# MLP handover, last attention units, and the layer-1 attention loop with its projection in single matmuls and its last fold in halves

## The chip, the cores and the metric

The kernel runs on one core of a Trainium2 chip. The metric is the device time of one execution in microseconds (us). PE is the matmul engine, DVE (VectorE), ACT (ScalarE) and POOL (GpSimd) are the elementwise engines, and SP is the queue from which all DMAs are issued. Each engine runs its own instructions in a fixed order and waits on semaphores.

## The reference, cut to what matters

Two layers of a diffusion transformer over 1024 latent tokens and 256 context tokens, width 1024, in float32:

```
for layer in range(2):
    h_l, h_c = modulate(x, norm1), modulate(ctx, norm1)
    layer 0: y_c, y_l = ab_mixer(h_c, h_l)        # mLSTM + windowed attention
    layer 1: y_l = c_mixer(h_c, h_l)              # full attention, 8 heads, 2 kv heads
    x = x + mod_l[2] * y_l
    x = x + mod_l[5] * (relu(modulate(x, norm2) @ w1) ** 2 @ w2)
    layer 0 only: the same two steps for ctx
return x

c_mixer:  q, k = rms_norm(q), rms_norm(k); rope for the latent ones
          k_all = [k_ctx, k_lat]; v_all = [v_ctx, v_lat]          # 1280 keys
          o = softmax(q k_all^T / sqrt(128)) v_all; y_l = o @ w_out
```

## The kernel before, in words

**High and low parts.** Every float32 operand of PE is kept as a rounded high part and the rest, its low part. `split` makes them: ACT copies the high part (L397), then DVE or POOL subtracts it from the source (L398). A product is three matmuls: high x high, high x low, low x high. A weight tile lands in a raw buffer by DMA and is then split into one of the buffers `W0_105`, `W1_106`, `W2_4594` to `W5_4597`.

**The MLP.** Both matrix products use a seven-product scheme on 2 x 2 blocks of operands. In the first one, `pair` computes two 128-wide hidden blocks from seven products (11, S1, 12, S2, 22, S3, S4). DVE combines the products out of PSUM (L643, "evacuations"), ACT applies the squared relu (`finish`, L600 and L601), and the results and sums of them go to DRAM (`hd`): `column_sums` and `row_sums` add blocks on DVE (L618) and store them (L619). `direct` (two matmul groups and a finish) does the context tokens of layer 0. Pairs 14 and 15 are in an order written out by hand. In the last pair the generator `ahead` is stepped once per `step()`: it loads and splits the operands of the first three steps of the second product, on POOL. This is the handover. `pending["row"]` holds the row sums of a pair; they run in the next pair, and their stores must land before their buffers are used again by that pair.

**The second product**, `mlp_out`, walks the hidden blocks in four stages ("14", "56", "27", "3"). A step is 24 matmuls (L1046) on operands that `mlp_feed` loads ahead (L924), adds (L969) and splits on DVE. The scheduler orders this part by its own model of time. The residual `x` is loaded from `xs` two tiles per step (L1119) and results are added to it on DVE (L1051).

**Layer 1's attention.** A unit is one head h and one tile t of 256 query tokens; 32 units run in an order written out by hand, and each iteration k works on three units: scores and maxima of k, values of k-1, division of k-2. Scores of the 1280 keys fill five PSUM banks of 512 columns (two chunks of 256 keys each, L423 to L425 through `mm3`). DVE folds them into a running maximum u.m, 512 wide (L1965), and at last merges its two halves (L1968). Two PE transposes (L1992), a reduction (L1994), two more transposes (L1998) and an ACT copy (L2002) bring the negative maximum to the layout of the scores; `shift` adds it (L2008). `weigh` takes the exponential on ACT (L2027 high part, L2028 in full) and the low part on POOL (L2029). `values` multiplies by V (L2017) into a bank that the chain of transposes uses too, so it waits for L2002. The sum of the exponentials is collected in ACC (`total1` copies on ACT, L1976; `total2` and `total3` add on DVE), `total4` sums it over partitions on PE (L2020), `divide1` takes its reciprocal by Ln and Exp on ACT (L2033, L2034), and `divide2` multiplies (L2038). Between these PE runs the query projection of unit k+2 as filler: `project` is a generator of 24 matmuls (L1924), and `run(fill, n)` takes n steps of it. The order on PE around it is

```
on(fold, k, 4, NB); fill = project(k + 2); run(fill, 5)
on(maxima1, k); run(fill, 2)
on(maxima2, k); on(total2, k - 1); run(fill, 2)
on(shift, k); on(values, k - 1, 0)
```

**The end of attention.** In the last six units `early` starts the output projection: it loads output weights (`load_wo`) and finished heads (`load_first`, from DRAM), splits them (`split_wo` on POOL, `split_first` on DVE or POOL) and runs their products as filler (`out`, L2079). Its table is keyed by unit (counted from the end) and place in the unit: -6 is k = 26, -1 is k = 31, and 0 and 1 are the two iterations after it.

## Time and profile before

| | us |
|---|---|
| three runs | 2779.29, 2780.57, 2788.60 |
| median | 2780.57 |
| the profiled execution | 2788.63 |
| its span, first to last instruction | 2786.8 |
| PE busy | 2695.9 (97%) |
| DVE, ACT, POOL busy | 1885.0, 1476.7, 1095.2 |
| mean granted PE clock | 0.992 |

Rows of a timeline have the start, the duration, engine, line, operation, names and shapes, a count, and in brackets the idle time ahead of it and what ended it. Layer 0's handover lies near 1200 to 1222 us, layer 1's attention loop between 1690 and 2068, layer 1's handover near 2472.

### The profile page before, as it was taken

The numbers are of one execution on the slowest core, as the hardware profiler recorded it, in microseconds if no ns is written. First come the engines' busy times: TensorE is split into PE (matmuls) and PEld (weight loads), VectorE is DVE, ScalarE is ACT, GpSimd is POOL, SyncE is SP. The second block draws the span as 40 slices with busy tenths as digits, with TensorE's granted clock in tenths as the row PEclk, the third lists the DMA queues.
The fourth block names the chain that finished last, engine by engine and source line by source line (L and its number), as shares of the span: only waits on it lengthen the run. The fifth ranks groups of instructions, "written<-read, shape, count | busy, mean of one in ns | idle before, by whom it ended". The sixth has DMA issues, their size and how long they took to land.

```text
span 2786.8 us, 40782 instructions
## 1 busy us (share of the span) xinstructions
PE 2695.9 (97%) x14683; PEld 2284.5 (82%) x14683; DVE 1885.0 (68%) x3268; ACT 1476.7 (53%) x2611; POOL 1095.2 (39%) x744
## 2 busy tenths in 40 slices
PE   6899999999999999999999999999999999999999
PEld 3688788878788888878878889999988888888877
DVE  4645655677876766557678757888874677666676
ACT  4654554445564444344436557888865554444432
POOL 3430220000237576530001346787865499740000
PEclk9999999999999999999999999999999999999999
DMA  7122233363335667488756710000045155577664
GB/s 241 56 84 100 79 104 112 108 210 99 110 108 174 209 220 237 157 307 286 246 166 218 243 61 26 24 28 20 26 150 195 65 174 192 175 284 263 215 223 154
DMA packets 194659, 428.33 MB, mean 154 GB/s; under 512 B 21128, under 2 KB 47336, under 8 KB 194456
## 3 DMA queue, kind: packets, MB, share of 16 engines
q1 hardware_dynamic: 194456, 425.73, 45.6%
q8 instruction: 115, 1.88, 0.3%
q14 instruction: 88, 0.72, 0.1%
HBM read 322.90 MB, written 102.74 MB: 153 GB/s over the span
## 4 chain that ended last, share of the span: by engine, by line
PE 73%; DVE 6%; DMA 4%; issue 3%; ACT 2%; POOL 1%; DVEq 0%; SPq 0%; POOLq 0%; ACTq 0%
PE psum L588 21%; PE psum L1046 17%; PE psum L423 4%; PE psum L2017 4%; PE psum L424 4%; PE psum L425 4%; PE psum L2203 3%; PE psum L1142 3%; PE psum L1924 3%; DMA hhiraw<-in_w 2%; DVE W L398 2%; POOL W L398 1%; PE psum L1500 1%; PE psum L2079 1%; PE psum L1506 1%
## 5 line engine op out<-in xcount | busy, mean ns | idle before, releaser
L398 POOL TENSOR_TENSOR W<-F,W 128x512 fp32r<-128x512 f32 (+2 forms) x319 | 489.1, 1547 | 519.4 <-ACT W L397 438.8
L1046 PE MATMUL psum<-W,W 128*128 128x512 f32 x2688 | 617.8, 391 | 10.9 <-DVE W L398 4.7
L1046 PEld LDWEIGHTS psum<-W,W 128*128 128x128 f32 x2688 | 504.6, 188 | 123.6 <-DVE W L398 10.9
L588 PE MATMUL psum<-hhi,W 128*128 128x512 f32 (+1 forms) x1600 | 442.2, 356 | 2.3 <-DVE x L1774 0.9
L397 ACT ACTIVATE W<-F 128x512 fp32r<-128x512 f32 (+2 forms) x380 | 275.1, 739 | 292.6 <-POOL F L561 99.4
L588 PEld LDWEIGHTS psum<-hhi,W 128*128 128x128 f32 x1600 | 285.1, 189 | 46.3 <-issue 2.5
L588 PE MATMUL psum<-hlo,W 128*128 128x512 f32 (+1 forms) x800 | 284.3, 355 | 0.0
L397 ACT ACTIVATE W<-hhiraw 128x1024 fp32r<-128x1024 f32 x98 | 104.0, 1061 | 316.2 <-PE psum L1046 235.4
L423 PE MATMUL psum<-hhi,W 128*128 128x512 f32 (+1 forms) x624 | 232.8, 373 | 0.9 <-ACT F L1432 0.9
L424 PE MATMUL psum<-hlo,W 128*128 128x512 f32 (+1 forms) x624 | 227.3, 364 | 0.0
L425 PE MATMUL psum<-hhi,W 128*128 128x512 f32 (+1 forms) x624 | 227.1, 364 | 0.0
L969 DVE TENSOR_TENSOR hhiraw<-hhiraw 128x512 f32<-128x512 f32 x154 | 108.3, 712 | 108.4 <-DMA hhiraw<-in_w 107.6
L561 POOL TENSOR_TENSOR F<-F 128x512 f32<-128x512 f32 x112 | 164.8, 1471 | 13.5 <-DMA F<-in_w 4.5
L588 PEld LDWEIGHTS psum<-hlo,W 128*128 128x128 f32 x800 | 151.2, 189 | 21.4 <-issue 0.2
L390 POOL TENSOR_TENSOR hlo<-F,hhi 128x512 fp32r<-128x512 f32 (+1 forms) x24 | 27.4, 1144 | 347.6 <-ACT F L381 347.6
L398 DVE TENSOR_TENSOR W<-hhiraw,W 128x1024 fp32r<-128x1024 f32 x98 | 119.6, 1221 | 60.7 <-ACT W L397 58.2
L423 PEld LDWEIGHTS psum<-hhi,W 128*128 128x128 f32 x624 | 118.4, 190 | 21.3 <-ACT x L397 2.5
L424 PEld LDWEIGHTS psum<-hlo,W 128*128 128x128 f32 x624 | 118.5, 190 | 17.3 <-issue 2.2
L425 PEld LDWEIGHTS psum<-hhi,W 128*128 128x128 f32 x624 | 118.3, 190 | 17.3 <-issue 0.5
L588 PE MATMUL psum<-x,W 128*128 128x512 f32 x504 | 123.5, 389 | 0.0
L398 DVE TENSOR_TENSOR W<-hloraw,W 128x1024 fp32r<-128x1024 f32 x98 | 119.4, 1218 | 0.7 <-ACT W L397 0.7
L2203 PE MATMUL psum<-W,W 128*128 128x512 f32 (+1 forms) x408 | 109.5, 372 | 2.4 <-POOL W L398 1.5
(450 smaller groups left out, 6231.2 us busy)
## 6 DMA issues: line engine op xcount, KB each, us to landing
F<-in_w SPq DMA_DIRECT2D x104, 512.0 KB
hloraw<-hd SPq DMA_DIRECT2D x90, 512.0 KB
hhiraw<-in_w SPq DMA_DIRECT2D x72, 512.0 KB
hd<-F SPq DMA_DIRECT2D x142, 256.0 KB
hhiraw<-in_w SPq DMA_DIRECT2D x116, 256.0 KB
F<-in_ada_w SPq DMA_DIRECT2D x96, 256.0 KB
hd<-x SPq DMA_DIRECT2D x90, 256.0 KB
F<-in_win SPq DMA_DIRECT2D x33, 512.0 KB
```

What stands on the lines that cost most here:

```text
L397: nc.scalar.activation(hi, src, AF.Copy)
L398: eng.tensor_tensor(lo, src, hi.bitcast(F32), op=ALU.subtract)
L423: nc.tensor.matmul(ps, sh, mh, start=i == 0, stop=False)
L424: nc.tensor.matmul(ps, sh, ml, start=False, stop=False)
L425: nc.tensor.matmul(ps, sl, mh, start=False, stop=i == n - 1)
L561: add = lambda o, p, q, how: nc.gpsimd.tensor_tensor(o, p, q, op=how)
L588: nc.tensor.matmul(ps, w[i][:, p], B[j][k], start=first and j == 0 and m == 0, stop=last and j == 3 and m == 2)
L969: tt = lambda o, p, q, how: eng.tensor_tensor(o, p, q, op=how)
L1046: nc.tensor.matmul(bank(base + i), A[u][:, p], B[v], start=first and m == 0, stop=last and m == 2)
L1142: nc.tensor.matmul(bank(k), B[u][:, i * P : i * P + P], A[v][:, half], start=f == 0 and m == 0, stop=f == NFF - 1 and m == 2,)
L2017: nc.tensor.matmul(u.o[:, :QT], v[x], p[y], start=c == 0 and m == 0, stop=c == 2 * NB - 1 and m == 2)
L2203: self.nc.tensor.matmul(ps, x[:, c], y, start=first and m == 0, stop=last and m == 2)
```

## The change

It has five parts. (1) In pair 15 the row sums of pair 14 run before product S1 instead of after it. (2) In `ahead` the low parts of the first step's hidden operand and the whole split of the second step's weights go from POOL to DVE. (3) The loads of x keep their program order in SP's queue, and the loads of kind "3" are issued behind the last of them in layer 0. (4) In the attention loop the projection yields after each matmul, and the fills between fold, first transposes, second transposes and values are 11, 5 and 8 matmuls instead of 15, 6 and 3 (the ninth step of the last fill takes the square of the finished projection). The fold's last block is taken in two 256-wide halves before the merge, and `divide1` stands before `total1`. (5) In the last units `split_wo(0)` moves from the start of unit 27 to behind its shift; heads 5 and 6 are staged in a free part of F and loaded in unit 30, and head 5 is split there on POOL instead of on DVE in unit 31.

```diff
@@ pair
             step()
+            if b == NFF // 2 - 1:
+                pending.pop("row")()
             ps = bank()
             prod(ps, A["S1"], T1)
@@ ahead
-            feed.split_b(0, eng)
+            feed.split_b(0, nc.vector)
             feed.load_a(2)
             yield
             feed.load_b(1)
-            feed.split_a(1, eng)
+            feed.split_a(1, nc.vector)
@@ mlp_feed
-        def load(t, src):
-            nc.sync.dma_start(t if len(src.shape) == 2 else t.rearrange("p (k n) -> p k n", k=src.shape[1]), src)
+        def load(t, src, behind=False):
+            t = t if len(src.shape) == 2 else t.rearrange("p (k n) -> p k n", k=src.shape[1])
+            with self.tc.issue_after(fd.mark.ins) if behind and hc else nullcontext():
+                nc.sync.dma_start(t, src)
...
@@ mlp_out
-                        nc.sync.dma_start(self.x[j][:, t0 : t0 + n], save[:, j, t0 : t0 + n])
+                        feed.mark = self.tc.keep_in_program_order(
+                            nc.sync.dma_start(self.x[j][:, t0 : t0 + n], save[:, j, t0 : t0 + n])
+                        )
@@ project
-                yield
+                    yield
@@ fold
-            for b in range(b0, b1):
+            for b in range(b0, min(b1, NB - 1)):
                 nc.vector.tensor_tensor(u.m, u.S[:, b * 512 : b * 512 + 512], u.m, op=ALU.max)
             if b1 < NB:
                 return
+            for i in range(2):
+                m, c = u.m[:, i * QT : i * QT + QT], 2 * NB - 2 + i
+                nc.vector.tensor_tensor(m, u.S[:, c * QT : c * QT + QT], m, op=ALU.max)
             nc.vector.tensor_tensor(u.m[:, :QT], u.m[:, :QT], u.m[:, QT:], op=ALU.max)
@@ load_first
-                stage[j] = aw.tile([P, H], F32, tag="mix", bufs=2)
+                if j in (5, 6):
+                    stage[j] = self.F[:, 2 * PG + (j - 5) * H : 2 * PG + (j - 4) * H]
+                else:
+                    stage[j] = aw.tile([P, H], F32, tag="mix", bufs=2)
@@ early
-                (-5, 0): ((split_wo, 0), (load_first, 0, 1)),
+                (-5, 0): ((load_first, 0, 1),),
+                (-5, 2): ((split_wo, 0),),
...
-                (-2, 0): ((load_wo, 2),),
+                (-2, 0): ((load_wo, 2), (load_first, 5, 6)),
...
-                (-2, 2): ((split_first, 3, V), (split_first, 4, G), (load_first, 5, 6)),
+                (-2, 2): ((split_first, 3, V), (split_first, 4, G), (split_first, 5, G)),
...
-                (-1, 3): ((split_first, 5, V), (out, 0, (5,))),
+                (-1, 3): ((out, 0, (5,)),),
@@ the loop
+                on(divide1, k - 2)
                 on(total1, k - 1)
-                on(divide1, k - 2)
...
-                run(fill, 5)
+                run(fill, 11)
...
-                run(fill, 2)
+                run(fill, 5)
                 on(maxima2, k)
                 on(total2, k - 1)
-                run(fill, 2)
+                run(fill, 9)
```

Three places in the order of instructions. First PE in an attention unit, from the last of the projection's matmuls ahead of the first transposes to the values. Before:

```order
6836 L1924 MATMUL psum<-hhi,W_4597 128x256
6837 L1992 MATMUL psum<-ident,F 128x128 x2
6838 L1924 MATMUL psum<-hhi,W_4597 128x256
6839 L1924 MATMUL psum<-hlo,W_4597 128x256
6840 L1924 MATMUL psum<-hhi,W_4597 128x256 x2
6841 L1924 MATMUL psum<-hlo,W_4597 128x256
6842 L1924 MATMUL psum<-hhi,W_4597 128x256
6843 L1998 MATMUL psum<-ident,F 128x128 x2
6844 L1924 MATMUL psum<-hhi,W_4597 128x256
6845 L1924 MATMUL psum<-hlo,W_4597 128x256
6846 L1924 MATMUL psum<-hhi,W_4597 128x256
6847 L2017 MATMUL psum<-x_13158,x_12916 128x256
```

In the changed kernel, whose line numbers are a few higher:

```order
6792 L2001 MATMUL psum<-ident,F 128x128 x2
6793 L1930 MATMUL psum<-hhi,W_4597 128x256 x2
6794 L1930 MATMUL psum<-hlo,W_4597 128x256
6795 L1930 MATMUL psum<-hhi,W_4597 128x256 x2
6796 L2007 MATMUL psum<-ident,F 128x128 x2
6797 L1930 MATMUL psum<-hlo,W_4597 128x256
6798 L1930 MATMUL psum<-hhi,W_4597 128x256 x2
6799 L1930 MATMUL psum<-hlo,W_4597 128x256
6800 L1930 MATMUL psum<-hhi,W_4597 128x256 x2
6801 L1930 MATMUL psum<-hlo,W_4597 128x256
6802 L1930 MATMUL psum<-hhi,W_4597 128x256
6803 L2026 MATMUL psum<-x_13158,x_12916 128x256
```

Five matmuls of the projection moved from ahead of the second transposes to behind them; four of them from ahead of the first.

Second DVE at layer 0's handover, from the evacuation of h11 of pair 15 (`x_7127` and `x_7126` are its temporaries, `W_105` and `W_106` operands of the second product). Before:

```order
1608 L643 TENSOR_TENSOR x_7127<-psum,x_7126 128x512
1609 L643 TENSOR_TENSOR x_7126<-psum,x_7126 128x512 x2
1610 L643 TENSOR_TENSOR x_7126<-x_7126,psum 128x512
1611 L643 TENSOR_TENSOR x_7126<-psum,x_7126 128x512
1612 L643 TENSOR_TENSOR F<-psum,x_7126 128x512
1613 L643 TENSOR_TENSOR x_7126<-psum,x_7126 128x512
1614 L618 TENSOR_TENSOR F<-x_7126,x_7127 128x512
```

In the changed kernel:

```order
1608 L643 TENSOR_TENSOR x_7127<-psum,x_7126 128x512
1609 L398 TENSOR_TENSOR W_105<-F,W_105 128x1024
1610 L643 TENSOR_TENSOR x_7127<-psum,x_7127 128x512
1611 L643 TENSOR_TENSOR x_7126<-psum,x_7126 128x512
1612 L973 TENSOR_TENSOR F<-F 128x512
1613 L398 TENSOR_TENSOR W_106<-F,W_106 128x1024
1614 L643 TENSOR_TENSOR x_7126<-x_7126,psum 128x512
1615 L643 TENSOR_TENSOR x_7126<-psum,x_7126 128x512
1616 L643 TENSOR_TENSOR F<-psum,x_7127 128x512
1617 L643 TENSOR_TENSOR x_7127<-psum,x_7127 128x512
```

Two low parts and an add came from POOL and stand between the evacuations of S2 (rows 1610 and 1611) and that of product 22 (row 1614).

Third POOL in units 29 to 31 (`hlo` is the low part of a finished head, `W_4597` an output weight). Before:

```order
468 L398 TENSOR_TENSOR hlo<-F,hhi 128x512
469 L2029 TENSOR_TENSOR x_13160<-x_13163,x_13158 128x1280
470 L1941 TENSOR_TENSOR F<-F 128x256
471 L1942 TENSOR_TENSOR F<-F 128x256
472 L2029 TENSOR_TENSOR x_13161<-F,x_13159 128x1280
473 L398 TENSOR_TENSOR W_106<-F,W_105 128x256
474 L398 TENSOR_TENSOR hlo<-F,hhi 128x512
475 L2029 TENSOR_TENSOR W_106<-x_13162,W_105 128x1280
476 L398 TENSOR_TENSOR W_4597<-F,W_4597 128x1024
```

In the changed kernel:

```order
465 L398 TENSOR_TENSOR hlo<-F,hhi 128x512
466 L2038 TENSOR_TENSOR x_13160<-x_13163,x_13158 128x1280
467 L1947 TENSOR_TENSOR F<-F 128x256
468 L1948 TENSOR_TENSOR F<-F 128x256
469 L2038 TENSOR_TENSOR x_13161<-F,x_13159 128x1280
470 L398 TENSOR_TENSOR W_106<-F,W_105 128x256
471 L398 TENSOR_TENSOR hlo<-F,hhi 128x512 x2
472 L2038 TENSOR_TENSOR W_106<-x_13162,W_105 128x1280
```

POOL splits a second finished head (x2) ahead of the low part of a unit's weights.

8 lines of the change are left out of this document (4 added, 4 removed).

## The prediction

> **What bounds the kernel now.** First the busy rows, then windows by stage, then PE's waits.
>
> ```profile
> PE 2695.9 (97%) x14683; PEld 2284.5 (82%) x14683; DVE 1885.0 (68%) x3268; ACT 1476.7 (53%) x2611; POOL 1095.2 (39%) x744
> ...
> 1200.00:1222.00 22.00, 16.55 (x72) 12.88 (x71) 11.62 (x13) 11.05 (x17) 13.11 (x7) 0.84 0.73 248
> 1222.00:1244.00 22.00, 22.00 (x99) 18.22 (x98) 15.32 (x16) 9.18 (x10) 1.67 (x1) 1.00 1.03 388
> 1712.00:2000.00 288.00, 284.46 (x2244) 275.41 (x2243) 249.66 (x391) 235.05 (x373) 226.98 (x152) 1.00 0.08 25
> ...
> PE psum L1046 <- DVE W L398: 4.7, 8, 0.9
> PE psum L1046 <- POOL W L398: 1.1, 1, 1.1
> ```
>
> PE bounds it: the change removes no matmul, so only PE's pauses can move. Columns of the windows: length, then busy time of PE, PEld, DVE, ACT, POOL, the granted clock. Layer 0's handover (1200 to 1222) lacks 5.5 us of PE and runs at clock 0.84; the 22 us behind it lack none (99 matmuls, 0.222 us each). The attention loop lacks 3.5 us in 288 (24 units of some 12 us); what its last units lack stands with term 2. The two wait rows are layer 1's output stage (4.7 us) and its handover (1.1).
>
> **Term 1, the attention loop.** One ordinary unit (last score matmul at S = 1947.27), then a unit near the end with no projection, whose chain nothing covers:
>
> ```profile
> 1947.27 0.28 PE L425 MATMUL psum<-W,hb 128*128 128x256 f32 x1
> 1947.47 0.41 DVE L2038 TENSOR_TENSOR F<-psum,F 128x256 f32<-128x256 f32 x1
> 1947.81 0.68 DVE L1965 TENSOR_TENSOR F<-psum,F 128x512 f32<-128x512 f32 x1
> 1948.52 0.43 DVE L1968 TENSOR_TENSOR F<-F 128x256 f32<-128x256 f32 x1
> 1949.19 0.39 PE L1992 MATMUL psum<-ident,F 128*128 128x128 f32 x2
> 1949.58 2.95 POOL L2029 TENSOR_TENSOR x<-x,x 128x1280 fp32r<-128x1280 f32 x1 [1.67 <-ACT x L2028]
> 1950.12 0.40 PE L1998 MATMUL psum<-ident,F 128*128 128x128 f32 x2
> 1950.56 0.38 ACT L2002 ACTIVATE F<-psum 128x256 f32<-128x256 f32 x1 [0.75 <-PE psum L1998]
> 1950.99 0.98 PE L2017 MATMUL psum<-W,x 128*128 128x256 f32 x6
> ...
> 2044.31 0.42 DVE L1968 TENSOR_TENSOR F<-F 128x256 f32<-128x256 f32 x1
> 2044.88 0.41 PE L1992 MATMUL psum<-ident,F 128*128 128x128 f32 x2 [0.16 <-DVE F L1968]
> 2045.82 0.41 PE L1998 MATMUL psum<-ident,F 128*128 128x128 f32 x2
> 2046.71 0.74 PE L2017 MATMUL psum<-x,x 128*128 128x256 f32 x4 [0.47 <-ACT F L2002]
> ...
> 1908.36 0.42 DVE L1985 TENSOR_TENSOR F<-psum,F 128x256 f32<-128x256 f32 x1
> 1908.82 0.42 DVE L1986 TENSOR_TENSOR F<-psum,F 128x256 f32<-128x256 f32 x1
> ```
>
> Now PE fills exactly up to the transposes: 16 starts in 1.92 us (0.12 each) reach the first at S+1.92, six more and two transposes (0.93, so the pair costs 0.21) the second at S+2.85. Only before the values does it pause: three more would reach them at S+3.42, they start at S+3.72, and the second one 0.22 later instead of 0.12 (six last 0.98, the last of them 0.28), S+3.94. The bare chain: merge L1968 to transpose 0.57, to the second transpose 0.94, to the values 0.89.
>
> The halves begin where the fold did, S+0.54. A 256-wide operation lets an independent one start 0.34 later (L2038 to L1965) and a dependent one 0.46 later (L1985 to L1986). The merge starts at S+1.34 instead of 1.25: two starts cost 0.80 where one cost 0.71. The transpose can start at S+1.91; PE, now with 11 matmuls ahead of it, is there at S+1.44 and pauses 0.47. Behind it five matmuls and two transposes (0.81) don't cover the chain's 0.94: second transposes at S+2.85. Two transposes and eight matmuls then lead to S+4.02, past the chain (2.85 + 0.89 = 3.74), so the old pause is gone; the second value matmul starts at S+4.14. Against S+3.94 that is +0.20 a unit: one pause of 0.3 and its slow restart are exchanged for two of 0.47 and 0.13. I take this value because the rows behind it are of the same shape, engine and operands. Lower end: with the merge at S+1.14, 0.11 earlier than now, the second value matmul is at S+3.94 again, nothing lost. Upper end: the 0.10 of a slow restart after the new pause, +0.30.
>
> The Trainium skill (VectorE: DVE Perf Modes, The TRN2 errata) says that each instruction pays a fixed extra latency, a large tile once and small tiles each; its PSUM row, (120 + elements)/0.96 GHz, gives as an estimate 0.66 us for 512 and 0.39 for 256, +0.12 a unit against the +0.09 of the rows, which would add about 1 us to the loop's sum. The trace's 0.68 and 0.41 agree within 0.03.
>
> The swapped reciprocal: L2033 waits for the total's matmul, and L1976 filled that wait.
>
> ```profile
> 1945.53 0.59 PE L2020 MATMUL psum<-F,ones 128*128 128x256 f32 x2
> 1945.69 0.58 ACT L1976 ACTIVATE psum<-x 128x512 f32<-128x512 f32 x1
> 1946.22 0.36 ACT L2033 ACTIVATE F<-psum 128x256 f32<-128x256 f32 x1
> ...
> 1913.91 1.35 ACT L397 ACTIVATE W<-F 128x256 fp32r<-128x256 f32 x2
> 1915.16 0.36 ACT L2002 ACTIVATE F<-psum 128x256 f32<-128x256 f32 x1
> ```
>
> The total ends at 1946.12, so L2033 can't move up, and L1976 behind L2034 costs ACT its 0.53 less 0.05 of idle: 0.48. Queued behind it: both weigh exponentials, then POOL's L2029, then L2002. In ordinary units ACT idles 0.75 before L2002, which covers it; without that cover it would cost 0.48 there too. In the six units that split the next head's weights (t = 3, heads 0 to 5) L2002 follows L397 at once: +0.48 there. Loop: 22 x 0.20 + 6 x 0.48 = **+7.3**; ends 0 and, with 0.30, +9.5. Two units without projection only see the later merge, 2 x 0.09: **+0.2**.
>
> **Term 2, the last units.**
>
> ```profile
> 2006.89 2.40 POOL L398 TENSOR_TENSOR W<-F,W 128x1024 fp32r<-128x1024 f32 x1
> 2008.07 1.50 DVE L1968 TENSOR_TENSOR F<-F 128x256 f32<-128x256 f32 x1
> 2009.69 0.20 PEld L1992 LDWEIGHTS psum<-ident,F 128*128 128x128 f32 x2 [1.55 <-ACT F L2028]
> ...
> 2056.83 0.41 PE L1992 MATMUL psum<-ident,F 128*128 128x128 f32 x2 [0.16 <-DVE F L1968]
> 2057.74 2.96 DVE L398 TENSOR_TENSOR hlo<-F,hhi 128x512 fp32r<-128x512 f32 x1
> 2060.76 0.79 PE L2079 MATMUL psum<-hlo,W 128*128 128x512 f32 x1 [2.49 <-DVE hlo L398]
> 2062.87 1.01 PE L2017 MATMUL psum<-W,x 128*128 128x256 f32 x3 [0.47 <-ACT F L2002]
> ```
>
> In unit 27 the merge takes 1.50 instead of 0.43 beside POOL's weight split; PE waits 1.55. Moved behind the shift, that split (one ACT and one POOL instruction) mostly lies in POOL's idle time (1.67 us of it before one of a unit's two L2029 above), and its weights are needed only units later: **-1.5**. In unit 31 a split on DVE takes 2.96 beside POOL, and first transpose to values lasts 6.04 where unit 30 took 1.83: with chunk 5 split a unit earlier on POOL, PE finds it done: **-4.2**. What is late next is L2002, as in unit 30. If the cover is gone (POOL behind with its second split of that unit, or the staging in F holding up the output weight that used to be loaded there) half of the gain stays: ends -5.9 and -3. The two staging loads, moved up SP's queue, pass only mix and output-weight loads; I cost them at nothing, since the loop moves 25 GB/s.
>
> **Term 3, layer 0's handover.**
>
> ```profile
> 1201.13 1.89 DVE L643 TENSOR_TENSOR x<-psum,x 128x512 f32<-128x512 f32 x3 [6.71 <-DMA hd<-x]
> 1203.78 1.05 ACT L397 ACTIVATE W<-F 128x1024 fp32r<-128x1024 f32 x1
> 1207.66 3.11 PE L1046 MATMUL psum<-W,W 128*128 128x512 f32 x12
> 1212.62 1.04 ACT L397 ACTIVATE W<-F 128x1024 fp32r<-128x1024 f32 x1
> 1213.73 2.35 POOL L398 TENSOR_TENSOR W<-F,W 128x1024 fp32r<-128x1024 f32 x1 [1.66 <-ACT W L397]
> 1216.14 6.23 PE L1046 MATMUL psum<-W,W 128*128 128x512 f32 x16 [1.93 <-POOL W L398]
> L398 DVE TENSOR_TENSOR W<-hhiraw,W 128x1024 fp32r<-128x1024 f32 x98 | 119.6, 1221 | 60.7 <-ACT W L397 58.2
> ```
>
> Two of POOL's splits (2.35 us each) and an add go to DVE, where a split takes 1.22. But DVE's order now has them ahead of pair 15's evacuations, and each waits for ACT. The h11 evacuation at 1201.13 waited for the store of a row sum; the row sums come earlier now and no x loads stand behind them, so I move all that follows up by 0.6. ACT's high part of W_105 then ends at 1204.2, DVE's low part at 1205.5, the two evacuations queued behind it at 1206.7, the add at 1207.4, ACT's next high part at 1208.4, DVE's low part at 1209.7, and the evacuation of product 22 only at 1210.4. PE needs that one's bank after three matmuls: a pause of 2.6. Behind it come the evacuations of S3 and S4 (till 1212.3), and behind these ACT's finishes, W_4597's high part till 1215.4 and POOL's low part till 1217.8, which is later than the 1216.1 of now. By then 27 of the first 48 matmuls are done, where now 13 are. Now the other 35 end at 1216.1 + 35 x 0.222 + 2.4 (the slow clock: 16 recorded ones take 6.23) = 1226.3; then, 21 more end at 1217.8 + 4.7 = 1222.5, 3.8 earlier. But the pair after that needs two more low parts from POOL, ready at 1225.2, and PE waits 1.8 of the gain back: **-2.0**. Ends -8.9 (5.5 of idle, 2.4 of slow clock and 1 of slow restarts: no loss left) and +2 (the pauses add and the clock falls).
>
> The granted clock falls to 0.84 after pauses of 2.9 and 1.9 us. By the Trainium skill (TensorE: Matmul & The Clock Gate, Part 1: The HAM clock gate (the "warmup" mystery)) the clock halves after an idle window of about 3.4 us, so pauses of 2.6 and 1.5 with 4 us of work between would keep it full; if it fell anyway, 2.4 comes back and the term is +0.4.
>
> **Term 4, the rest.** Layer 1's handover loses its 1.1 to POOL but gets the same blocked evacuations: **-0.5**, ends -1.1 and +3. The x loads, two in each step of 24 matmuls (5.3 us), are all issued before the first stage ends; nothing. In the output stages DVE's 4.7 us may shift either way by 2.
>
> **Sum**: 7.3 + 0.2 - 1.5 - 4.2 - 2.0 - 0.5 = -0.7. Against the profiled execution (2788.6, of which the span is 2786.8) that is 2787.9; it lies 8.0 above the runs' median of 2780.6 and is as long as the longest of them. A difference carries over, so 2780.6 - 0.7, **2780**.
>
> **Rivals.** *Shorter chain*: the halves let the merge start early. At S+1.14 the loop costs nothing (2780 - 7.3 = 2772.7), at S+0.87 PE waits for no merge, the second value matmul is at S+3.67, and 28 x 0.27 comes off (2765). For: half the fold needs only the first score chunk. Against: DVE, not the scores, sets the start, S+0.54. *Free handover*: evacuations don't block, all 8.9 us come back: 2773. Against: DVE runs in order. *ACT late everywhere* (slower): the slip of 0.48 pushes L2029, ending at S+5.26, towards the second half of the values, which needs it at S+4.02 + 15 x 0.12 + 0.33 = S+6.15. It decides from a slip of 0.9; each 0.1 beyond costs 28 x 0.1, so 1.2 gives 2788. For: POOL is busy 227 of 288 us. Against: a slip of 0.48 leaves 0.41. *The moves earn nothing*: DVE waits for the store as before, and POOL or the staging is late in the last units; terms 2 and 3 are zero: 2780 + 7.7 = 2788. Against: both waits end on the instructions that are moved.
>
> **Numbers.** Forecast 0.54 (alone 2774 to 2785), shorter chain 0.14, free handover 0.12, ACT late 0.10, no earnings 0.10. A measurement of this kernel tells about 0.3%, 8.4 us, from no change. Faster: 0.14 and half of 0.12, 0.20; slower: 0.06 of ACT late, 0.04 of no earnings, 0.04 of the forecast's tail, 0.14; same 0.66. Range 2768 to 2789: it takes in the ends of terms 1 and 3 taken singly and all the rivals but the chain with no pause left and the worst slips; about 0.15 lies outside.
>
> **What would show it.** In the changed kernel's line numbers. Term 1: PE pauses before each unit's first transposes (L2001) and not before its values (L2026), the merge (L1977) at S+1.34, the period 0.2 longer. Term 2: no merge of 1.5 us in unit 27, unit 31's chain under 2 us. Term 3: DVE's two L398 stand ahead of evacuations, PE waits for DVE near 1208 and for POOL near 1216. The prediction is wrong if the merge starts before S+1.2, if PE waits for L2038 (the low parts of the weights), or if the handover runs without a pause.

## The result: slower by a quarter of a per cent

| | before | changed |
|---|---|---|
| median, 10 runs each (us) | 2782.38 | 2790.24 |
| lowest and highest | 2778.03, 2789.10 | 2786.68, 2793.05 |
| the profiled execution, and its span | 2788.63, 2786.8 | 2789.22, 2787.4 |
| mean granted PE clock | 0.992 | 0.994 |

The ratio is 1.0025 with a 95% interval of 1.0013 to 1.0036: the change costs 3.6 to 10 us, most likely 7. I had forecast 2780 within 2768 to 2789, a difference of -0.7 us. The time lies 1.2 us above the range, and the difference is too large to be none, though it is smaller than the 0.3% that I had called a change. Of the distance from 2780 to 2790, 1.8 us lie in the kernel before, whose ten runs have their median at 2782.38 where the three that I had gave 2780.57; the rest is the change.

From the page of the changed kernel the busy row:

```profile
PE 2694.0 (97%) x14683; PEld 2281.7 (82%) x14683; DVE 1895.7 (68%) x3305; ACT 1482.4 (53%) x2611; POOL 1087.8 (39%) x739
```

Three windows of it, with the columns of the prediction's windows (length; busy time of PE, PEld, DVE, ACT, POOL; granted clock):

```profile
1200.00:1222.00 22.00, 19.02 (x85) 15.02 (x84) 14.42 (x16) 12.81 (x19) 6.96 (x4) 0.92 0.76 254
1222.00:1244.00 22.00, 19.57 (x79) 15.97 (x80) 14.12 (x14) 7.69 (x8) 2.38 (x1) 0.92 1.03 386
1712.00:2000.00 288.00, 279.65 (x2197) 268.93 (x2197) 245.85 (x406) 234.15 (x364) 223.59 (x150) 1.00 0.08 24
```

The waits of PE that answer to those of before (in the changed kernel L1050 is the second product, L2001 the first transposes, L1977 the merge, L2026 the values, L2029 the sum over partitions):

```profile
PE psum L2001 <- DVE F L1977: 12.5, 32, 1.1
PE psum L2029 <- DVE F L1995: 2.7, 2, 2.0
PE psum L1050 <- DVE x L643: 2.4, 1, 2.4
```

The attention loop now lacks 8.3 us of PE in 288 where it lacked 3.5, and every one of the 32 units waits for its merge. The window of layer 0's handover lacks less than before (3.0 instead of 5.5), but the 22 us behind it, which lacked nothing, now lack 2.4 and run at clock 0.92. (The windows stand still in time, while the second product starts 2.1 us earlier in this profile, so they don't cover quite the same instructions; the table below does.)

To see where the time went, the program is cut at instructions that all kernels share. "Layer 0, 300" is the time from the first to the 300th matmul of layer 0's second product, "rest" what follows to its last one; S of a unit is the start of its last score matmul, as in the prediction; "to next" runs from S of unit 31 to the first matmul of the next product of three (L423) behind the attention. Layer 1's first product ends at the first matmul of its second.

| us | before, two profiles | changed | difference |
|---|---|---|---|
| first matmul of layer 0's second product | 1207.66, 1201.38 | 1205.52 | same program |
| layer 0, 300 | 75.75, 75.71 | 77.37 | +1.6 |
| layer 0, rest | 239.94, 239.57 | 237.73 | -2.0 |
| units 0 to 2 | 21.79, 21.79 | 22.30 | +0.5 |
| units 2 to 27 | 295.30, 295.25 | 302.13 | +6.9 |
| units 27 to 31 | 48.73, 48.69 | 49.07 | +0.4 |
| unit 31 to next | 36.07, 35.40 | 33.24 | -2.2 to -2.8 |
| layer 1, first product | 311.08, 311.08 | 311.60 | +0.5 |
| layer 1, 300 | 69.33, 69.38 | 69.93 | +0.6 |
| layer 1, rest | 243.19, 242.55 | 240.81 | see below |

### The profile page after: what moved, and what is told of

The parts are those of the page before. It is cut to its first block, busy times and chain, and to the rows that moved or that the text cites. A ratio compares the mean times of both kernels' runs of the same rounds, so it can differ in the third digit from the quotient of the medians.

```text
span 2787.4 us, 40823 instructions
## 1 busy us (share of the span) xinstructions
PE 2694.0 (97%) x14683; PEld 2281.7 (82%) x14683; DVE 1895.7 (68%) x3305; ACT 1482.4 (53%) x2611; POOL 1087.8 (39%) x739
## 4 chain that ended last, share of the span: by engine, by line
PE 70%; DVE 7%; ACT 4%; DMA 4%; issue 3%; POOL 1%; SPq 0%; DVEq 0%; POOLq 0%; ACTq 0%
PE psum L588 22%; PE psum L1050 16%; PE psum L423 4%; PE psum L424 4%; PE psum L425 4%; PE psum L2026 4%; PE psum L2216 3%; PE psum L1148 3%; DMA hhiraw<-in_w 3%; DVE W L398 2%; PE psum L1930 2%; POOL W L398 1%; PE psum L1506 1%; DVE F L1976 1%; ACT W L397 1%
## 5 line engine op out<-in xcount | busy, mean ns | idle before, releaser
L398 POOL TENSOR_TENSOR W<-F,W 128x512 fp32r<-128x512 f32 (+2 forms) x315 | 481.4, 1543 | 536.7 <-ACT W L397 459.6
L1050 PE MATMUL psum<-W,W 128*128 128x512 f32 x2688 | 617.0, 391 | 9.7 <-POOL W L398 4.6
L1050 PEld LDWEIGHTS psum<-W,W 128*128 128x128 f32 x2688 | 505.7, 189 | 120.7 <-POOL W L398 5.9
L423 PE MATMUL psum<-hhi,W 128*128 128x512 f32 (+1 forms) x624 | 233.0, 373 | 0.0
L398 DVE TENSOR_TENSOR W<-hhiraw,W 128x1024 fp32r<-128x1024 f32 x98 | 121.9, 1244 | 73.4 <-ACT W L397 72.8
L423 PEld LDWEIGHTS psum<-hhi,W 128*128 128x128 f32 x624 | 118.6, 190 | 20.3 <-ACT x L397 2.5
L398 DVE TENSOR_TENSOR W<-hloraw,W 128x1024 fp32r<-128x1024 f32 x98 | 122.9, 1254 | 4.0 <-DMA hhiraw<-in_w 4.0
```

The costliest lines, as they stand in the source:

```text
L398: eng.tensor_tensor(lo, src, hi.bitcast(F32), op=ALU.subtract)
L423: nc.tensor.matmul(ps, sh, mh, start=i == 0, stop=False)
L1050: nc.tensor.matmul(bank(base + i), A[u][:, p], B[v], start=first and m == 0, stop=last and m == 2)
```

## The experiments

Each kernel's stage times are gathered here; the text below names the column. "Both", "none", "one" tells how many of the handover's two low parts are on DVE.

| kernel | low parts on DVE | layer 0, 300 | rest | units 2 to 27 | 27 to 31 | to next | time (us), runs | ratio to before, 95% |
|---|---|---|---|---|---|---|---|---|
| e0_before | none | 75.71 | 239.57 | 295.25 | 48.69 | 35.40 | 2780.51, 1 | |
| e1_loop | none | 75.08 | 240.03 | 302.01 | 50.23 | 37.02 | 2793.16, 5 | 1.0037 (1.0025 to 1.0050) |
| e2_noloop | both | 78.18 | 237.99 | 295.08 | 47.42 | 32.71 | 2779.99, 11 | 0.9983 (0.9973 to 0.9993) |
| e3_pool | none | 75.21 | 238.03 | 302.07 | 49.02 | 33.23 | 2780.69, 1 | |
| e4_fills | both | 77.32 | 237.55 | 297.90 | 48.52 | 34.34 | 2782.46, 1 | |
| e5_nohalves | both | 79.66 | 237.55 | 301.25 | 48.67 | 34.31 | 2791.14, 1 | |
| e6_noswap | both | 79.46 | 237.55 | 299.33 | 48.83 | 32.72 | 2784.82, 1 | |
| e7_kept | none | 76.30 | 239.77 | 295.09 | 47.42 | 34.31 | 2780.11, 12 | 0.9988 (0.9977 to 1.0000) |
| e8_early | none | 75.11 | 237.77 | 296.55 | 50.26 | 33.60 | 2781.72, 11 | 0.9997 (0.9988 to 1.0006) |
| e9_loadq | none | 75.91 | 237.82 | 296.51 | 50.20 | 32.53 | 2784.28, 11 | 1.0002 (0.9993 to 1.0011) |
| e10_late | none | 75.28 | 237.58 | 295.19 | 47.41 | 31.27 | 2773.20, 1 | |
| e11_divide | none | 74.93 | 240.43 | 297.75 | 48.86 | 31.40 | 2780.96, 11 | 0.9986 (0.9977 to 0.9995) |
| e12_last | none | 75.75 | 239.83 | 295.13 | 47.43 | 31.27 | 2776.79, 11 | 0.9974 (0.9965 to 0.9983) |
| e13_b_dve | one | 72.48 | 237.55 | 295.01 | 48.60 | 31.26 | 2771.65, 1 | |
| e14_a_dve | one | 73.80 | 237.55 | 295.03 | 47.40 | 31.27 | 2771.13, 1 | |
| e15_best | one | 73.87 | 237.55 | 295.14 | 48.62 | 31.25 | 2773.47, 11 | 0.9972 (0.9962 to 0.9983) |

The medians were not taken on the same chips, so the ratios are to be compared and not the medians. The single times carry a spread of some 6 us that arises ahead of all these stages (e0_before shows it), so single runs are read by their stages alone.

**e0_before: the kernel before once more**, with no edit.

> The kernel before once more, for its stages. Theory (the profiled execution of before was a long one, 8 us above the median, and long in the stages that DMAs feed): an execution near 2781 us has the attention loop (unit 2 to unit 27) at 295.3 us to within 0.2, but the time up to layer 0's second product, the rest of that product, or layer 1's second product is shorter than in the first profile by 2 us each. Rival (the execution was long everywhere by a little, or the profile carries over term by term): every stage keeps its length to within 0.5 us.

Behind the first matmul of layer 0's second product the two profiles of one program agree within 2 us, and the loop within 0.05. Ahead of it they differ by 6.3 us, which is most of the 8.1 between their times (2788.63 and 2780.51). So the profile of before was long for a reason that no part of the change touches, and taking the difference over to the median was right. What differs there is told under what I had not expected.

**e1_loop: the kernel before with the loop's part alone.**

```diff
-                yield
+                    yield
...
+            for i in range(2):
+                m, c = u.m[:, i * QT : i * QT + QT], 2 * NB - 2 + i
+                nc.vector.tensor_tensor(m, u.S[:, c * QT : c * QT + QT], m, op=ALU.max)
...
-                run(fill, 5)
+                run(fill, 11)
-                run(fill, 2)
+                run(fill, 5)
-                run(fill, 2)
+                run(fill, 9)
```

(and `divide1` ahead of `total1`)

> Before with the loop's part alone: projection in single matmuls with fills 11, 5 and 8, the last fold in halves, divide1 ahead of total1. Theory (the loop is what costs): units 2 to 27 take 302.1 us as in the changed kernel instead of 295.3, and the kernel is slower than before by 7 to 8 us, near 2790. Rival (the loop costs little, and the handovers and moves cost the time): slower by at most 2 us.

Units 2 to 27 take 302.01: +6.7 for 25 units. Another +0.5 lies in the first two units and +2.5 to +3.1 in the last ones (27 to 31: +1.5, to next: +1.0 to +1.6). The ratio of 1.0037 is +10.3 us, and these three make 9.7 to 10.3. By these figures the loop's part alone costs more than the whole change (10.3 against 7), though the two intervals overlap.

**e2_noloop: the change without the loop's part** (the reverse of e1's diff on the changed kernel, the fills counted in single matmuls: 15, 6, 4).

> The changed kernel with the loop's part undone (fills 15, 6 and 3, one fold, total1 ahead of divide1); handovers and last units stay changed. Theory (the loop is what costs): units 2 to 27 back at 295.3 us, the whole within 3 us of before, since the last units give 3 to 4 us and the two handovers take 2 to 3 back. Rival (handovers and moves cost the time): still slower than before by 5 us or more.

The loop is back at 295.08. What is left is faster than before, -4.7 us (1.9 to 7.5): the last units give 1.3 and 2.7 to 3.4, the rest of layer 0's second product 1.6 to 2.0, and 2.4 is lost in the first 300 matmuls and 1.1 in layer 1 (311.62 and 69.89). e1's +10.3 and this -4.7 add to +5.6, within the interval of the whole change.

**e3_pool: the change with the handover's low parts back on POOL.**

```diff
-            feed.split_b(0, nc.vector)
+            feed.split_b(0, eng)
-            feed.split_a(1, nc.vector)
+            feed.split_a(1, eng)
```

> The changed kernel with the low parts and the add in the handover back on POOL; the earlier row sums and the order of the x loads stay. Theory (DVE's order blocks the evacuations, and PE's pauses bring a slow clock with them): from the first matmul of layer 0's second product to its 300th 75.8 us or less instead of 77.4, no pause of 2.6 us after three matmuls, and layer 1 at 69.3 instead of 69.9. Rival (the lost time comes from the stores and the x loads): both as in the changed kernel, within 0.3 us.

Layer 0's first 300 matmuls take 75.21 instead of 77.37, and layer 1 is back at 311.08 and 69.34: the move of the low parts costs both handovers. Over all kernels of the table, the ten with none on DVE (the profile of before with them) take 74.9 to 76.3, mean 75.5, and the five with both 77.3 to 79.7, mean 78.4. The move costs 2.9 us in layer 0 and 1.1 in layer 1, 4.0 in all.

**e4_fills, e5_nohalves, e6_noswap: one of the loop's three edits undone at a time.**

```diff
e4:  fills 11, 5, 9  ->  15, 6, 4
e5:  the last fold in one piece, 512 wide
e6:  total1 ahead of divide1 again
```

> The changed kernel with the fills back at 15, 6 and 3 matmuls; halves and the earlier divide1 stay. Theory (the fills are what costs in ordinary units: eight matmuls behind the second transposes are more than the chain needs, and the pause moves to the first ones): ordinary units back at a period of 11.75 us with PE waiting before the values only, the six units with a weight split keep their 0.48, so units 2 to 27 take 298.3 us (changed 302.1, before 295.3). Rival (the later merge costs, wherever the fills stand): 300.5 or more.

> The changed kernel with the last fold in one piece; fills and divide1 stay. Theory (a half costs the merge 0.07 us, no more): the merge starts 1.25 us behind the last score matmul, ordinary units 0.07 shorter than in the changed kernel, units 2 to 27 at 300.4 us. Rival (the halves cost most of the 6.8 us): 298 or less. Other rival (the halves shorten the chain, as half the fold needs only the first chunk): 303 or more.

> The changed kernel with total1 ahead of divide1 again. Theory (the earlier divide1 only costs the six units that split the next head's weights, where the values go back from 4.52 to 4.16 us): ordinary units as in the changed kernel, units 2 to 27 at 300.0 us. Rival (the slip of ACT costs every unit): 298 or less.

Against the changed kernel's 302.13 for units 2 to 27, undoing the fills gives back 4.2, the swap 2.8 and the halves 0.9. That adds to 7.9, a little over the 6.9 of all three. The largest single cause is the fills, and the overlap with the halves shows in one unit of e4_fills (S = 1943.67):

```profile
1944.99 0.42 DVE L1977 TENSOR_TENSOR F<-F 128x256 f32<-128x256 f32 x1
1945.59 0.38 PE L2001 MATMUL psum<-ident,F 128*128 128x128 f32 x2
```

The merge is as late as in the changed kernel, S+1.32, but with 15 matmuls ahead PE comes to the first transposes only at S+1.92 and doesn't wait, and an ordinary unit takes 11.75 us as before (changed: 11.96). So the halves cost something only where the four matmuls are gone from ahead of the first transposes: in e5_nohalves 0.07 in each ordinary unit and nothing in the units with t = 3 or the ones behind them, which makes 0.9 where I had expected 1.75. What is left in e4_fills, 2.7, is the swap's.

**e7_kept: the parts of the change that looked worth keeping**, that is, e2_noloop with e3's edit.

> The changed kernel without the loop's part and with the low parts of the handover back on POOL: what stays is the earlier row sums, the order of the x loads and the last units. Theory (these are the parts that gain): units 27 to 31 and on to the fifth output weight shorter by 4 us than before, layer 0's second product by 2, the handovers as before: faster than before by 6 to 9 us, near 2776. Rival (the x loads' order and the row sums only looked better in one profile): not more than 4 us faster.

The ratio of 0.9988 is about -3 us, less than I had expected. In its profile the unit 31 stage was disturbed by a phase at half clock (34.31, where e2_noloop has 32.71 with the same instructions), the rest of layer 0 took 239.77 instead of 237.6 to 238.0, and units 0 to 2 took 22.54 instead of 21.79, unit 1's merge lasting 0.83 instead of 0.43.

**e8_early, e9_loadq, e11_divide: moving `divide2` out from between the folds.** If the merge sets the unit, it should start earlier. e8 moves the sum over partitions up and `divide2` ahead of the fold before, and keeps the reciprocal ahead of the copy; e9 also moves the next weights' split behind the shift; e11 puts `divide2` behind the merge. The fills differ too: 12, 6 and 6 matmuls in e8 and e9 and 13, 6 and 5 in e11, where before has 15, 6 and 3.

```diff
e8:  -                on(fold, k, 1, 4)
     +                on(fold, k, 1, 3)
                      on(divide2, k - 2)
     +                on(fold, k, 3, 4)
                      on(fold, k, 4, NB)
e11: -                on(fold, k, 1, 4)
     +                on(fold, k, 1, NB)
                      on(divide2, k - 2)
     -                on(fold, k, 4, NB)
```

> e7_kept (loop, fills and folds of before; only the moved row sums, x loads and last units of the change) with a loop of my own: the column sum of the unit before last (total4) moves up behind the third scores block and the reciprocal ahead of the copy, so that divide2 (0.33 us on DVE) leaves the place between the last two folds; the single-matmul fills are 12, 6 and 7. Theory (the chain fold, merge, transposes, maximum, transposes, copy sets the unit wherever the 24 fill matmuls do not cover it, so what counts is when the merge starts): merge at S+1.06 instead of S+1.25, values 0.3 earlier in each ordinary unit, none in the six units whose ACT splits the next weights; units 2 to 27 take 288 to 290 us (295.3 in the kernel before, 302.1 in the changed one), whole kernel 2770 to 2774. Rival (total4 is now early and waits on DVE for total3, and the scores behind it wait with it): no gain, 295 or more, 2780.

> e8_early with the next head's weight load and split (load_q) moved behind the shift, so that ACT's copies of the query weights stand behind the copy of the maximum (L2002 in the kernel before) and not ahead of it. Theory (the six units with this split are held by ACT): each gains 0.4 and the other units nothing, units 2 to 27 take 2 to 2.5 us less than in e8_early. Rival (the weights then come too late for the projection, or ACT's copies delay the exponentials of the same unit, which the values need one unit later): same as e8_early or up to 3 us more.

> e7_kept with divide2 behind the merge (so no other DVE instruction stands between the folds), single-matmul fills of 13, 6 and 6, and the two moves of e10_late with the fourth output-weight load kept behind the second split. e8_early left the start of the last fold at S+0.56 because divide2 only moved into a DVE queue that was already full behind the third scores block. Theory (what counts is when the merge starts, and DVE is free enough behind it): last fold at S+0.32, merge at S+1.05 instead of S+1.25, values 0.3 earlier in the units without a head split and without POOL beside the merge: units 2 to 27 take 288 to 290 us (295.09 in e7_kept), the last units 1.5 less than in e7_kept and e2_noloop, whole kernel 2772 to 2776 against 2782.5 of before. Rival (PE is the bound there, since three fill matmuls fewer ahead of the transposes only move the pause; or divide2 now stands ahead of the maximum's reduction): 294 to 296 us, whole kernel 2779 to 2782.

All three miss: 296.55, 296.51 and 297.75, each a little slower than the 295.1 of the loop of before. The timeline of e8_early, whose unit has S = 1947.38 (L1971 is the fold, L2044 `divide2`, L1974 the merge):

```profile
1946.26 0.69 DVE L1971 TENSOR_TENSOR F<-psum,F 128x512 f32<-128x512 f32 x1 [0.48 <-PE psum L425]
1946.87 0.41 DVE L2044 TENSOR_TENSOR F<-psum,F 128x256 f32<-128x256 f32 x1
1947.20 1.48 DVE L1971 TENSOR_TENSOR F<-psum,F 128x512 f32<-128x512 f32 x2
1948.71 0.42 DVE L1974 TENSOR_TENSOR F<-F 128x256 f32<-128x256 f32 x1
```

From the third fold on, DVE has no idle time: fold, `divide2`, two folds and the merge follow one another from 1946.26, and it does not matter in which of these places `divide2` stands. The merge starts at S+1.33 instead of S+1.25. To leave, it would have to use the idle 0.48 ahead of this row, and ACT ends its reciprocal only at 1946.53. The same in e11_divide, S = 1949.90:

```profile
1949.50 1.49 DVE L1971 TENSOR_TENSOR F<-psum,F 128x512 f32<-128x512 f32 x2 [0.30 <-PE psum L425]
1951.03 0.43 DVE L1974 TENSOR_TENSOR F<-F 128x256 f32<-128x256 f32 x1
1951.37 0.42 DVE L2044 TENSOR_TENSOR F<-psum,F 128x256 f32<-128x256 f32 x1
1951.84 0.44 PE L1998 MATMUL psum<-ident,F 128*128 128x128 f32 x2
```

Here the merge does start earlier, S+1.12 instead of S+1.25, but PE's transposes start only at S+1.94, behind `divide2`: it reads the finished head out of the bank that the transposes write. The merge's gain is lost to a wait that the data demand. So in the places that ran the 0.33 us of `divide2` belong to the chain: the transposes can't start before S+1.90 in e8 and S+1.94 in e11, and in before, where PE doesn't hold them up (units 30 and 31), they start at S+1.83. That explains why nothing was gained. That something was lost is in e8 at least the fills' doing: with 12 matmuls ahead PE is at the transposes too early and pauses there, an ordinary unit takes 11.85 us, and in e4_fills, whose merge is as late, it takes 11.75 with 15 ahead. In e11 most of the loss lies in the units behind those with t = 3 (12.20 instead of 11.92), whose merge takes 0.81 instead of 0.67. No run has these orders with the fills of before. In e8 the units with t = 3 take 11.85 like the others, so e9 had nothing left to give there.

**e10_late: two more moves in the last units, on e7_kept.**

```diff
-                (-1, 0): ((split_wo, 1), (load_wo, 3)),
+                (-1, 0): ((load_wo, 3),),
-                (-1, 2): ((split_first, 6, V), (load_first, 7)),
+                (-1, 2): ((split_wo, 1), (load_first, 7)),
+                (0, 5): ((split_first, 6, V),),
```

> e7_kept with two more moves in the last units: POOL's second output-weight split goes from the start of unit 31 to behind its shift, and DVE's split of head 6 from behind that shift to the start of the next iteration, behind total3. Theory (the gain I had counted for the last units went to two waits behind the ones removed: unit 31's merge beside that POOL split, 1.22 instead of 0.43 us, and total4 of unit 30 behind the head split, 0.7 of DVE): unit 31's merge takes 0.43 again, total4 waits 0.7 less, and from unit 27 to the first scores of the last values the kernel takes 1.5 less than in e2_noloop and e7_kept (27 to 31: 47.42; 31 to the output products 32.7 without a slow clock). Rival (the split then stands ahead of POOL's low parts of the last exponentials and the values of unit 31 wait for it): the 0.8 at the merge comes back, but 1 to 2.4 are lost behind it, no change or worse.

In this kernel the fourth output weight's load comes ahead of the second one's split and takes its staging buffer, so one block of the output projection uses the wrong weights; the instructions are the same in number and shape. The last units take 47.41 and 31.27 together 78.7, 1.45 less than e2_noloop's 80.1, as expected. Unit 31's merge, its values and the sum over partitions of unit 30 in its timeline:

```profile
2048.59 0.42 DVE L1974 TENSOR_TENSOR F<-F 128x256 f32<-128x256 f32 x1
...
2052.51 2.42 POOL L398 TENSOR_TENSOR W<-F,W 128x1024 fp32r<-128x1024 f32 x1
...
2056.25 0.70 PE L2026 MATMUL psum<-F,ones 128*128 128x256 f32 x2 [1.39 <-DVE F L1992]
```

The merge takes 0.42 instead of 1.22 with POOL's split 3.9 us behind it, and PE waits 1.39 instead of 2.00 for the sum's operand.

**e12_last: e10's two moves with the load kept behind the split**, on e7_kept.

```diff
-                (-1, 0): ((split_wo, 1), (load_wo, 3)),
-                (-1, 2): ((split_first, 6, V), (load_first, 7)),
+                (-1, 2): ((split_wo, 1), (load_wo, 3), (load_first, 7)),
+                (0, 5): ((split_first, 6, V),),
```

> e7_kept (loop and handover engines of before; the change's row sums, x loads and last units) with the two moves of e10_late, the fourth output-weight load kept behind the second split. Theory (the handovers and the loop cost what the stage times said, and the last units gain once the two waits behind the removed ones are gone too): units 2 to 27 295.1, 27 to 31 47.4, from there to the output weight's products 31.3, layer 0's handover 75.3, layer 1's 311.1 and 69.35; 6 us of the last units and about 1 of the x loads: 2774 to 2777 against 2782.5 of before, ratio 0.9975. Rival (a slow-clock phase falls on the last units whatever the order, as in the kernel before and in e7_kept): 34 instead of 31.3, 2779.

The last units take 47.43 and 31.27 again, 5.4 to 6.1 less than in the two profiles of before. The ratio is 0.9974: 7.3 us faster than before (4.7 to 9.7), as expected. The gain that I had counted on in the x loads is absent in this run (rest 239.83).

**e13_b_dve and e14_a_dve: one low part on DVE, on e12_last.** `split_b(0)` is the low part of the first step's hidden operand (the expectation calls it the weights'), `split_a(1)` the add and low part of the second step's weights.

```diff
e13: -            feed.split_b(0, eng)
     +            feed.split_b(0, nc.vector)
e14: -            feed.split_a(1, eng)
     +            feed.split_a(1, nc.vector)
```

> e12_last with the low part of the first step's weights alone on DVE (split_b(0)); the hidden operand's add and low part stay on POOL. Theory (two evacuations queue behind that low part on DVE, but PE has no product ready for them yet): first matmul to the 300th of layer 0's second product 75.3, as with both on POOL, and layer 1's handover 311.1 and 69.35. Rival (the evacuations blocked by it carry the loss): 77.4 and, in layer 1, +0.5 ahead of its second product.

> e12_last with the add and the low part of the next step's operand alone on DVE (split_a(1)). Theory (the loss is the evacuation of product 22, which stands behind that low part and holds PE's next bank for 2.4 us): 77 to 78 for the first 300 matmuls of layer 0's second product, and +0.5 to +0.6 in layer 1's. Rival (the low part on DVE only fills what POOL would have filled): 75.3 and 69.35.

For layer 0 theory and rival fall in both. One on DVE is better than none or both: 72.48 and 73.80 against means of 75.5 and 78.4. In layer 1 e13 costs nothing (311.11 and 69.35), e14 costs 1.5 (311.61 and 70.32), so the price there is that of the second step's low part. From e13_b_dve's timeline, the two low parts and PE's stretches of the second product:

```profile
1202.10 1.23 DVE L398 TENSOR_TENSOR W<-F,W 128x1024 fp32r<-128x1024 f32 x1 [3.09 <-ACT W L397]
1203.04 2.55 POOL L398 TENSOR_TENSOR W<-F,W 128x1024 fp32r<-128x1024 f32 x1 [5.31 <-ACT W L397]
1204.86 1.10 PE L1050 MATMUL psum<-W,W 128*128 128x512 f32 x4
1207.56 2.11 PE L1050 MATMUL psum<-W,W 128*128 128x512 f32 x8 [1.61 <-DVE x L643]
1210.35 0.96 PE L1050 MATMUL psum<-W,W 128*128 128x512 f32 x3 [0.67 <-ACT W L397]
1212.78 3.48 PE L1050 MATMUL psum<-W,W 128*128 128x512 f32 x14 [1.47 <-POOL W L398]
```

POOL starts its low part before DVE has ended the other, no second one stands ahead of DVE's evacuations, and PE's three pauses (from start to start 1.77, 0.83 and 1.64 longer than between two matmuls at full clock) add to 4.24; with both on POOL the pauses add to 4.9 to 5.3, with both on DVE to 5.9 to 8.2.

**e15_best: e13_b_dve again, in eleven runs.**

> The kernel of e13_b_dve again (loop of before; the change's row sums, x loads and last units with the two later moves; of the handover's two low parts only that of the first step's weights on DVE), in full rounds. Theory (two engines make the two low parts side by side, and PE finds the third pair's ready): layer 0's first 300 matmuls in 72.5 us as in the single look, 3 us less than in e12_last, 2773 to 2775 against 2782.5 to 2784.5 of before, ratio 0.9964. Rival (the single look had a lucky start): no different from e12_last, ratio 0.9974.

The ratio is 0.9972, 7.8 us faster than before (4.7 to 10.6). That version beats both kernels, but its gain over e12_last (0.9974) isn't told apart by these runs. The first 300 matmuls took 73.87 with the same three pauses as e13, 1.4 more:

```profile
1203.48 1.08 PE L1050 MATMUL psum<-W,W 128*128 128x512 f32 x4
1206.19 2.11 PE L1050 MATMUL psum<-W,W 128*128 128x512 f32 x8 [1.62 <-DVE x L643]
1208.97 0.97 PE L1050 MATMUL psum<-W,W 128*128 128x512 f32 x3 [0.67 <-ACT W L397]
1211.41 4.91 PE L1050 MATMUL psum<-W,W 128*128 128x512 f32 x14 [1.47 <-POOL W L398]
```

The last stretch has the same 14 matmuls, which took 3.48 us there and 4.91 here: seven of them ran at half clock.

## Why the prediction was wrong

**Term 1, the loop: right.** Predicted for the 25 units from 2 to 27: 19 x 0.20 + 6 x 0.48 = 6.7; measured +6.8 to +6.9. An ordinary unit of the changed kernel, S = 1950.57 (L2047 is `divide2`, L1976 the folds, x2 the halves; the filler and ACT are left out):

```profile
1950.57 0.28 PE L425 MATMUL psum<-W,hb 128*128 128x256 f32 x1
1950.77 0.42 DVE L2047 TENSOR_TENSOR F<-psum,F 128x256 f32<-128x256 f32 x1
1951.10 0.75 DVE L1976 TENSOR_TENSOR F<-psum,F 128x256 f32<-128x256 f32 x2
1951.88 0.43 DVE L1977 TENSOR_TENSOR F<-F 128x256 f32<-128x256 f32 x1
1952.46 0.41 PE L2001 MATMUL psum<-ident,F 128*128 128x128 f32 x2 [0.29 <-DVE F L1977]
1954.61 0.88 PE L2026 MATMUL psum<-W,x 128*128 128x256 f32 x6
```

The merge starts at S+1.31 (predicted S+1.34), the transposes at S+1.89 (S+1.91), the values at S+4.04 (S+4.02). The pause stands before L2001 and not before L2026, as the last part of the prediction asked. An ordinary unit takes 11.96 us instead of 11.74. In the units with t = 3 the second value matmul comes at S+4.52, and these units take 12.31 instead of 11.83, +0.48 as predicted. e6_noswap gives back 2.8 us, close to 6 x 0.48, but not in that way: 0.35 in each of these units and 0.11 in each unit behind one. Only the ends of the loop were sized short: e1_loop puts 0.5 into the first two units and 2.5 to 3.1 into the last ones, where my terms had 0.8.

**Term 2, the last units: the sign was right, the size wrong.** Predicted -5.7. Measured -1.8 to -2.5 in the changed kernel, and -4.0 to -4.7 in e2_noloop, where the loop's own price isn't in it. The waits that I removed are gone: unit 31's chain from the first transposes to the values takes 1.83 us, as predicted, and unit 27's merge is short. The step that failed is the sentence "What is late next is L2002". Late next were two others. Unit 31 of the changed kernel (L398 on DVE is the split of head 6, L1995 the sum's last add):

```profile
2059.80 2.41 POOL L398 TENSOR_TENSOR W<-F,W 128x1024 fp32r<-128x1024 f32 x1
...
2061.27 1.22 DVE L1977 TENSOR_TENSOR F<-F 128x256 f32<-128x256 f32 x1
2062.64 0.41 PE L2001 MATMUL psum<-ident,F 128*128 128x128 f32 x2 [1.02 <-DVE F L1977]
2064.47 0.98 PE L2026 MATMUL psum<-W,x 128*128 128x256 f32 x6 [0.47 <-ACT F L2011]
2067.32 0.68 DVE L398 TENSOR_TENSOR hlo<-F,hhi 128x512 fp32r<-128x512 f32 x1
2069.84 0.42 DVE L1995 TENSOR_TENSOR F<-psum,F 128x256 f32<-128x256 f32 x1
2070.32 0.70 PE L2029 MATMUL psum<-F,ones 128*128 128x256 f32 x2 [2.00 <-DVE F L1995]
```

First, POOL's second output-weight split, pushed back by the head that POOL now splits ahead of it, runs beside the merge, which takes 1.22 instead of 0.43. I had priced a merge beside POOL's split for unit 27; for unit 31 I had named this split only as something that could halve the gain, not as a price on the merge. Second, PE waits 2.00 for the sum over partitions: from the values to that sum are 5.85 us. In the kernel before they are the same 5.85, from 2062.87 to the second of these rows (the first is its last value matmuls):

```profile
2066.23 2.56 PE L2017 MATMUL psum<-x,W 128*128 128x256 f32 x15
2068.72 0.70 PE L2020 MATMUL psum<-F,ones 128*128 128x256 f32 x2
```

There PE was as late as DVE: 20 value matmuls ran at half clock after the long pause, so the DVE chain behind them (shift, head split, adds) was hidden, and it became the bound as soon as PE was not slow. (In e0_before, where 11 ran at half clock, PE already waits 0.79 for it, and the stretch is 5.85 again.) The moved split of unit 27 in turn reached into unit 28, whose merge takes 0.97. e10_late and e12_last bear this out: with unit 31's merge short again and the wait for the sum cut from 2.00 to 1.39, the last units give 5.4 to 6.1, as much as the 5.7 of the term, though by two moves that the change doesn't have.

**Term 3, layer 0's handover: wrong in sign.** Predicted -2.0; measured +1.6 in this profile and +2.9 as the mean of the kernels with both low parts on DVE. The changed kernel's timeline, from the first low part on DVE; L398 on POOL makes first the low part of the second step's hidden operand, then (x2) the third step's two:

```profile
1202.77 1.23 DVE L398 TENSOR_TENSOR W<-F,W 128x1024 fp32r<-128x1024 f32 x1 [3.09 <-ACT W L397]
1205.52 0.86 PE L1050 MATMUL psum<-W,W 128*128 128x512 f32 x3
1206.92 1.23 DVE L398 TENSOR_TENSOR W<-F,W 128x1024 fp32r<-128x1024 f32 x1 [1.12 <-ACT W L397]
1208.80 7.33 PE L1050 MATMUL psum<-W,W 128*128 128x512 f32 x24 [2.42 <-DVE x L643]
1213.85 2.40 POOL L398 TENSOR_TENSOR W<-F,W 128x1024 fp32r<-128x1024 f32 x1 [22.16 <-ACT W L397]
1216.31 5.32 PE L1050 MATMUL psum<-W,W 128*128 128x512 f32 x22 [0.19 <-POOL W L398]
1218.69 5.69 POOL L398 TENSOR_TENSOR W<-F,W 128x1024 fp32r<-128x1024 f32 x2 [1.18 <-ACT W L397]
1218.79 3.39 DVE L398 TENSOR_TENSOR W<-hhiraw,W 128x1024 fp32r<-128x1024 f32 x1
1224.43 3.80 PE L1050 MATMUL psum<-W,W 128*128 128x512 f32 x11 [2.80 <-POOL W L398]
```

The chain came as worked out up to the third pair of low parts: PE pauses 2.59 after three matmuls for the evacuation of product 22 (predicted 2.6), and POOL's low part ends 10.74 us after the first matmul (predicted 10.74). Two sizes failed. The first is a wait: the step "The pair after that needs two more low parts ... PE waits 1.8 of the gain back" was 1.8 and measured 2.95 here and 3.0 to 4.1 in the four other kernels with both on DVE: POOL's two low parts ran against DVE's next ones, and took 5.69 together, where the same two took 4.76 in e14_a_dve, while DVE's took 3.39 instead of 1.22. The second is the clock: it fell, though every pause was shorter than 3: seven matmuls at half clock at 1209.3 and seven at 1226.3, 3.5 us with the slow restarts, where the term had none. The first seven filled most of the wait for POOL before the second pair, which shrank from the predicted 1.5 to 0.35. So from -2.0 the account of this profile is +1.15 for the longer pause, +3.5 for the clock and -1.15 for the filled wait, which makes +1.5 against the measured +1.6. The prediction had taken the idle window that the Trainium skill (TensorE: Matmul & The Clock Gate, Part 1: The HAM clock gate (the "warmup" mystery)) gives as about 3.4 us as a reason why the clock would stay up, and had the other case at +0.4; the trace doesn't bear that use of it out: here half clock followed pauses of 2.59 and 2.95. The earlier row sums, which the term let move everything up by 0.6, don't show behind the first matmul: the first 300 take 75.5 on average in the seven kernels that have them with both low parts on POOL, and 75.5 in the three profiles that have neither edit. And neither side of the comparison that the term made is the best: one low part on each engine is better than both on DVE or both on POOL.

**Term 4, the rest.** Layer 1's handover was to give 0.5 and costs 1.1 (+0.5 ahead of the second product, +0.6 in its first 300 matmuls); the wait of 1.1 on POOL that was to go came back as pauses of 0.5 and 1.8 behind the blocked evacuations. The x loads, costed at nothing, seem to give 2 us in the rest of layer 0's second product: 239.6 to 240.0 in the three profiles without them, 237.6 to 238.0 in twelve of the fifteen with them, and 239.8 to 240.4 in the other three (e7_kept, e11_divide, e12_last). The 2 us are pauses of PE of 0.2 to 0.8 in front of single steps between 1410 and 1450 us; PE waits there for DVE's low parts, and DVE had waited for a load (in e7_kept 1.80 and 2.03 ahead of two of them). The three issue their loads in the same order as e8_early to e10_late, which hardly have these pauses, so it differs from run to run whether the loads are late, and that the new order makes it rarer is likely by these counts but not shown. Layer 1's output stage took 240.8 in the changed kernel, but also 241.1 in e1_loop, which has before's code there, so I don't count its 2 us to the change.

**The sum.** Loop 6.9, the first units 0.5, last units -2.1, layer 0's handover 2.9 (the mean), x loads -2.0, layer 1's handover 1.1: +7.3, where the ratio says +7 (3.6 to 10). The sum mixes one profile's stages with a mean and takes the x loads' 2.0 in full, so it agrees better than it could be relied on to. The forecast had 7.5 - 5.7 - 2.0 - 0.5 = -0.7. So the term that costs was right to 0.2 in the loop itself, and of the three that were to pay 8.2 for it one paid 4.0 to 4.7 (2.5 of it lost again to the loop's price in the same units) and the other two, in the mean, cost 4.0. Of the rivals, *the moves earn nothing* came nearest (2788), not through its mechanism, since both waits did move, but because each was followed by another.

## What to carry to other kernels

Where a stall is removed, ask of every engine, not only of the next one in the same chain, what had been hidden behind it: here a stall and the half clock after it had covered a chain on DVE that was just as long. When work moves from a slow engine to a fast one that runs in order, price what queues behind it, and try the split between both before moving all. And if a term that costs is certain and the terms that are to pay for it each rest on "late next", weigh them as less than their sum.
